# Router logits taken from rows that are not yet normalised, with gates, tables and tile addresses moved

## The chip, the core and the metric

The kernel runs on one core of one Trainium2 chip. The metric is device time in microseconds (us), the median over runs; lower is better. Five engines work in parallel from their own in-order queues: TensorE (PE in the profile, its weight loads PEld), VectorE (DVE), ScalarE (ACT), GpSimd (POOL) and SyncE (SP), which here issues the weight transfers.

## What is computed

256 tokens of width 1024 in float32 go through two blocks. Shortened from the reference:

```python
h = layer_norm(ALPHA * x + hybrid_mixer(x), ln1_g, ln1_b)        # first block
logits = h @ router_w + router_b                                 # 32 experts
top_vals, top_idx = lax.top_k(logits, 4); gates = softmax(top_vals)
# each expert: up (1024 -> 2048), gated activation, down (1024 -> 1024), for its tokens
h = layer_norm(ALPHA * h + moe(h), ln2_g, ln2_b)
u = rmsnorm(h)                                                   # second block
h = h + hybrid_mixer_2(u)   # projections, a scan over chunks of 128 with decays per head
h = h + conv_gated_mlp(rmsnorm(h)); return rmsnorm(h)
# the decays of the scan, for each of 32 heads:
decay_in = exp(where(causal, a_cum[l] - a_cum[s], -inf))
```

## The kernel before

**Projections.** Each float32 product is made of three matmuls (`mm3`, L163 to L165): activations and weights are split into a high and a low part, and high-high, high-low and low-high are added in PSUM. ACT rounds the high part of a weight chunk (tile wh, L61), DVE or POOL subtracts for the low one (wl, L158). In `units_t` a unit is 128 output columns: the weights are stationary and the 256 tokens stream past. In `units_n` it is the other way round. Activations lie in pairs of tiles: xth/xtl, soh/sol and hq/hk in the first mixer; uth/utl, xT, utx/yl0, ln/bc and yah/yal in the second block. `drive` runs the units in the order of a written list, and after every unit `tick` lets one side task (hgrn, attention, ssd, ...) take a step, up to its next `yield`.

By the built program, units_t issues 864 such matmuls with xth/xtl streaming, 192 with soh/sol and hq/hk, 1752 with uth/utl, 384 with xT, 384 with utx/yl0 and ln/bc, and 1056 with yah/yal; units_n issues 384 in the first mixer (w_out) and 192 in the second (w_o), and the last down projection 264 of 512 columns. The program also tells where each tile begins in a partition's memory. Modulo 512 bytes: the tiles wh and wl at 448 in the first mixer, at 64 in the second block; xth/xtl, soh/sol and hq/hk at 448; uth/utl, xT, utx and ln at 192; yl0, bc, yah and yal at 0. Of all the pairs that a matmul reads, only yah/yal with wh/wl have the activations at 0 and the weights at 64.

**Router.** The last units of the first mixer (w_out) end in `on_out` (L694, L696), which adds the residual to the rows xs block by block (256 columns) and takes statistics. `route` then normalises the rows (L789), transposes them on PE (L797), applies gain and bias (L800), multiplies by the router weights (L807), folds the four partial sums (L823) and picks the top four (L831 to L838). Three matmuls (L840 to L842) turn the choice into positions (L845), from which DVE builds a one-hot (L1059). The rows are split in hh and hl (ACT, and POOL at L816), and `gather` (L1021) multiplies them with the one-hot.

**Experts.** `some(0, 16)` and `some(16, 32)` go through the experts, 4 up chunks and 2 down chunks of 2 MB each, streamed by SP into eight slots: six of the rings and two of the tile lp, which also holds ln1's rows and the transposed rows while `route` runs, so that the second lp slot is handed over after it. After expert 0's up matmuls (L969) come `gates` (L858 to L877) and the slots of expert 0 (L987 to L992); `overflow_tables` (L889 to L936) follows as a side task from expert 1. `between(k)` runs after each of the eight k of an up projection; at k = 1 it issues the transposes of the expert before (`act_t`, L960), the sum into the result (`combine`, L1008) and the next slots.

**Decays.** In `ssd_near`, for each head, PE multiplies a one-hot column (selh, 64 partitions) with the running sums (ahl, 64 partitions: high and low part), 384 columns (L1437), and adds a mask (L1438) before ACT takes the exponent.

Of the kernel before, what the change touches and what calls it, by code (L numbers as in the profile page):

```python
# [28 lines left out]
P = 128  # L29
# [392 lines left out]
def mixer_1(g, xs, st, params, more, then):  # L422
# [3 lines left out]
    with ExitStack() as c:  # L426
# [6 lines left out]
        pa = c.enter_context(tc.tile_pool(name="m1pa", bufs=4, space=PSUM))  # L433
        lv = q.tile([P, 7, P], F32)
# [256 lines left out]

        def on_out(j, pt):
            s = slice(j, j + T)
# [4 lines left out]
        first = list(ut(2048, 512, on_hf))  # L698
        gates_u = [*ut(3584, 1024, copy_to(gs)), *ut(4608, 1024, copy_to(gh))]
        drive(g, [first[0], own, *first[1:], *ut(1536, 512, on_hq), *ut(3072, 512, on_hg),  # L700
                  lambda: g.tasks.append(hgrn()),
                  *un(1024, 512, copy_to(vs, False)), step, *un(2560, 512, copy_to(hv, False)), step,
                  *ut(512, 512, copy_to(sk)), step, *ut(0, 512, copy_to(sq, scale=0.125)), step,
                  *gates_u[:2], start_sb, *gates_u[2:],
# [3 lines left out]
                  *units_n(g, A["w_out"][0], 0, D, mg, sp, pj, on_out)], then)  # L708

# [6 lines left out]
def moe_params(g, p, land, pa):  # L716
# [24 lines left out]
    r.gb = turn_rows(g, rows, n, p, pa, "gb")  # L741
    r.b_up = p.tile([P, D], F32R, name="bup")
# [4 lines left out]
    r.fold = p.tile([P, NE], F32, name="fold")  # L747
    nc.vector.tensor_reduce(r.fold, g.ident.rearrange("p (r e) -> p e r", r=4), axis=mybir.AxisListType.X, op=OP.add)
# [4 lines left out]
    r.ones = p.tile([P, P], F32, name="ones")  # L753
    nc.vector.memset(r.ones, 1.0)
# [14 lines left out]
def route(g, h, st, lp, p, pu_, pd_, pc_):  # L769
# [4 lines left out]
    ln = lp[:, WIDE:WIDE + 2 * D].rearrange("p (a d) -> p a d", a=2)  # L774
    gam, bet = bcast_row(g, ln[:, 0], "ln1_g"), bcast_row(g, ln[:, 1], "ln1_b")
    hT = lp[:, WIDE + 2 * D:].rearrange("p (k t) -> p k t", k=8)
    add_ring(g, lp, 0, 1, WIDE)
    n = len(g.ahead)
    g.ahead += [fetch(g, *src) for src in (up_src(A, 0) + up_src(A, 1))[n:n + 1]]
    r.hh = p.tile([P, 2, D], F32R, name="hh")  # L780
    r.hl = p.tile([P, 2, D], F32R, name="hl")
    mv = p.tile([P, 2, 3], F32, name="mv")
    for tt in range(2):
        nc.vector.bn_aggr(mv[:, tt, :2], st[:, tt])
    rsqrt(g, mv[:, :, 2:3], mv[:, :, 1:2], 1e-5)
    for b in range(4):
        s = slice(b * T, b * T + T)
        for tt in range(2):
            nc.vector.tensor_scalar(h[:, tt, s], h[:, tt, s], mv[:, tt, 0:1], mv[:, tt, 2:3],  # L789
                                    op0=OP.subtract, op1=OP.mult)  # L790

    pl = pd_.tile([P, T], F32, name="pd")
    for b in range(4):
        pt = pu_.tile([P, 4, T], F32, name="pu")[:, :2] if b % 2 else pc_.tile([P, 2, T], F32, name="pc")
        for k in (2 * b, 2 * b + 1):
            for tt in range(2):
                nc.tensor.transpose(pt[:, k % 2, tt * P:tt * P + P], h[:, tt, k * P:k * P + P], g.ident)  # L797
        for k in (2 * b, 2 * b + 1):
            if k in (3, 5, 7):
                nc.vector.tensor_scalar(hT[:, k], pt[:, k % 2], r.gb[:, k:k + 1], r.gb[:, 8 + k:9 + k],  # L800
                                        op0=OP.mult, op1=OP.add)
            else:
                g.act(hT[:, k], pt[:, k % 2], AF.Identity, scale=r.gb[:, k:k + 1], bias=r.gb[:, 8 + k:9 + k])
        for k in (2 * b - 2, 2 * b - 1) if b < 3 else range(4, 8):
            if k >= 0:
                q = k % 4 * NE
                nc.tensor.matmul(pl[q:q + NE], r.rw[:, k], hT[:, k], start=k < 4, stop=k >= 4,  # L807
                                 skip_group_check=True, tile_position=(0, q))

    hv = h.rearrange("p t (q k) -> p t k q", k=8)  # L810
    hhv, hlv = (x.rearrange("p t (k q) -> p t k q", k=8) for x in (r.hh, r.hl))
    for b in range(2):
        s = slice(b * 4, b * 4 + 4)
        for tt in range(2):
            g.act(hhv[:, tt, s], hv[:, tt, s], AF.Copy)
            nc.gpsimd.tensor_sub(hlv[:, tt, s], hv[:, tt, s], hhv[:, tt, s])  # L816
    nc.gpsimd.tensor_mul(h[:, 0], h[:, 0], gam)
    nc.gpsimd.tensor_add(h[:, 0], h[:, 0], bet)
    lT = p.tile([P, 4 * P], F32, name="lT")[:, :T]
    nc.vector.tensor_copy(lT, pl)  # L820
    lg = pd_.tile([P, 2, NE], F32, name="pd")
    for tt in range(2):
        nc.tensor.matmul(lg[:, tt], lT[:, tt * P:tt * P + P], r.fold, start=True, stop=True)  # L823
    L = p.tile([P, 2, NE], F32, name="L")
    nc.vector.tensor_add(L, lg, r.rb[:, None, :].to_broadcast([P, 2, NE]))
# [1055 lines left out]
```

## Time and profile before

| | |
|---|---|
| median of 3 runs | 1806.98 us (1804.88 to 1809.86) |
| profiled execution | 1805.9 us, its span 1804.1 us |
| PE busy | 1680.7 us, 93% of the span |
| DVE, ACT, POOL busy | 42%, 31%, 9% |
| 244 to 266 us (router) | PE 12.60 of 22 us, granted clock 0.76 of full |
| 385 to 740 us (experts) | PE 329.49 of 355 us, transfers at 425 GB/s |
| 1225 to 1330 us (second block) | PE 101.35 of 105 us, DVE 72.86 |
| 1422 to 1638 us | PE 208.14 of 216 us, DVE 142.14 |
| 1638 to 1804 us | PE 158.58 of 166 us, DVE 98.55 |

The first mixer runs to 244 us, the router to 266, the experts to about 1208, the second block to the end. Busy is the time an engine spends in instructions; matmuls overlap, so that their rate is read from the distances between their starts.

### The profile page before, as it was taken

How to read it: one execution, taken by the hardware profiler on the slowest of the kernel's cores; microseconds unless marked ns; L12 is line 12 of the kernel's file. 1: busy time of each engine (PE TensorE's matmuls, PEld its weight loads, DVE VectorE, ACT ScalarE, POOL GpSimd, SP SyncE). 2: the span in 40 equal slices, each digit the busy share in tenths (PEclk: the TensorE clock that was granted, in tenths of full speed). 3: DMA queues.
4: the chain of work that ended last, by engine and by line, in shares of the span. 5: the costliest groups of instructions: out<-in, count | busy, mean ns of one | idle time of the engine just before them, and what ended most of it. 6: DMA issues, size and time to landing. Idle time of an engine off the chain costs nothing.

```text
span 1804.1 us, 23870 instructions
## 1 busy us (share of the span) xinstructions
PE 1680.7 (93%) x10102; PEld 1077.5 (60%) x10102; DVE 749.7 (42%) x1154; ACT 554.5 (31%) x858; POOL 158.2 (9%) x120
## 2 busy tenths in 40 slices
PE   6999979999999999899999999989999999999998
PEld 6998853333333333333333333348998899998997
DVE  4765462212211212122122121246766757566665
ACT  4547431010010100101001011016665456345454
POOL 4311230000000000000000000015201300021000
PEclk9999988999999999899999999999999999999999
DMA  9440858999999999899999999994543355545552
GB/s 304 132 149 16 309 210 328 424 418 428 428 427 427 428 428 427 375 428 427 427 428 429 425 428 428 427 334 131 185 141 117 118 187 187 168 165 170 193 183 92
DMA packets 149933, 535.60 MB, mean 297 GB/s; under 512 B 7123, under 2 KB 119139, under 8 KB 125504
## 3 DMA queue, kind: packets, MB, share of 16 engines
q1 hardware_dynamic: 147488, 529.68, 75.0%
q0 software_dynamic: 2048, 4.23, 0.7%
q8 instruction: 80, 1.31, 0.3%
q14 instruction: 29, 0.24, 0.0%
q10 hardware_dynamic: 288, 0.13, 0.0%
HBM read 532.97 MB, written 1.05 MB: 296 GB/s over the span
## 4 chain that ended last, share of the span: by engine, by line
PE 50%; DVE 4%; issue 2%; ACT 1%; POOL 1%; DMA 0%; DVEq 0%; ACTq 0%; POOLq 0%
PE pu L969 13%; PE pj L163 7%; PE pj L165 7%; PE pj L164 7%; PE pd L978 6%; PE pc L1008 2%; PE pa L164 1%; PE pa L165 1%; PE pa L163 1%; DVE xs L1010 1%; PE pc L1021 1%; POOL wl L158 1%; PE pa L1437 1%; PE px L960 1%; PE pu L1074 1%
## 5 line engine op out<-in xcount | busy, mean ns | idle before, releaser
L969 PE MATMUL pu<-ring,xt 128*64 128x512 f32 x1568 | 362.2, 613 | 1.3 <-ACT xt L61 1.3
L158 DVE TENSOR_TENSOR wl<-ring,wh 128x1024 fp32r<-128x1024 f32 (+1 forms) x224 | 269.8, 1228 | 51.5 <-ACT wh L61 51.2
L61 ACT ACTIVATE wh<-ring 128x1024 fp32r<-128x1024 f32 (+1 forms) x247 | 252.1, 1027 | 97.9 <-PE pj L164 41.7
L969 PEld LDWEIGHTS pu<-ring,xt 128*64 128x64 f32 x1568 | 110.3, 141 | 215.4 <-issue 208.9
L1010 DVE TENSOR_TENSOR xs<-xs,pc 128x512 f32<-128x512 f32 x124 | 79.7, 683 | 336.9 <-PE pc L1008 336.9
L947 DVE TENSOR_SCALAR xg<-pu 128x512 f32<-128x512 f32 x32 | 22.1, 691 | 360.1 <-PE pu L969 360.1
L163 PE MATMUL pj<-uth,wh 128*128 128x256 f32 x584 | 166.8, 286 | 0.0
L165 PE MATMUL pj<-uth,wl 128*128 128x256 f32 x584 | 164.8, 282 | 1.9 <-DVE wl L158 1.9
L164 PE MATMUL pj<-utl,wh 128*128 128x256 f32 x584 | 164.4, 281 | 0.0
L158 POOL TENSOR_TENSOR wl<-ring,wh 128x1024 fp32r<-128x1024 f32 x22 | 58.4, 2656 | 1105.2 <-ACT wh L61 1082.0
L978 PE MATMUL pd<-ring,act 128*64 128x512 f32 x704 | 154.8, 592 | 0.0
L61 ACT ACTIVATE sg<-xg 128x512 f32<-128x512 f32 x32 | 20.1, 630 | 350.8 <-DVE xg L947 350.8
L1008 PE MATMUL pc<-y,gpt 64*128 64x512 f32 x248 | 89.1, 645 | 24.9 <-DVE xs L1010 24.0
L165 PEld LDWEIGHTS pj<-uth,wl 128*128 128x128 f32 x584 | 110.0, 188 | 2.5 <-DVE wl L158 2.5
L163 PEld LDWEIGHTS pj<-uth,wh 128*128 128x128 f32 x584 | 110.0, 188 | 2.2 <-issue 2.1
L978 PEld LDWEIGHTS pd<-ring,act 128*64 128x64 f32 x704 | 50.4, 137 | 100.7 <-issue 100.7
L969 PE MATMUL pu<-lp,xt 128*64 128x512 f32 x480 | 110.4, 609 | 0.0
L164 PEld LDWEIGHTS pj<-utl,wh 128*128 128x128 f32 x584 | 110.0, 188 | 0.1
L163 PE MATMUL pj<-yah,wh 128*128 128x256 f32 x352 | 97.6, 277 | 0.0
L164 PE MATMUL pj<-yal,wh 128*128 128x256 f32 x352 | 97.4, 277 | 0.0
L165 PE MATMUL pj<-yah,wl 128*128 128x256 f32 x352 | 97.4, 277 | 0.0
L163 PE MATMUL pj<-xth,wh 128*128 128x256 f32 x288 | 84.3, 293 | 8.7 <-ACT wh L61 8.7
(440 smaller groups left out, 2853.4 us busy)
## 6 DMA issues: line engine op xcount, KB each, us to landing
ring<-in_expert_w_up_dram SPq DMA_DIRECT2D x98, 2048.0 KB, 19.9
ring<-in_expert_w_down_dram SPq DMA_DIRECT2D x44, 2048.0 KB, 18.4
ring<-in_w_in_dram SPq DMA_DIRECT2D x62, 1024.0 KB, 5.4
lp<-in_expert_w_up_dram SPq DMA_DIRECT2D x30, 2048.0 KB, 17.9
lp<-in_expert_w_down_dram SPq DMA_DIRECT2D x18, 2048.0 KB, 19.8
ring<-in_w_up_dram SPq DMA_DIRECT2D x22, 1024.0 KB, 5.2
ring<-in_w_down_dram SPq DMA_DIRECT2D x11, 1024.0 KB, 4.9
ring<-in_w_s_out_dram SPq DMA_DIRECT2D x8, 1024.0 KB, 5.0
```

What stands on the lines that cost most here:

```text
L61: self.nc.scalar.activation(out, x, func, **kw)
L158: return (hi_t, lo_t), lambda: (engine or g.nc.vector).tensor_sub(lo_t, src, hi_t)
L163: nc.tensor.matmul(out, a[0][asl], b[0][bsl], start=first, stop=False, skip_group_check=True)
L164: nc.tensor.matmul(out, a[0][asl], b[1][bsl], start=False, stop=False, skip_group_check=True)
L165: nc.tensor.matmul(out, a[1][asl], b[0][bsl], start=False, stop=last, skip_group_check=True)
L947: nc.vector.tensor_scalar(xg, pv[:, :, 0], 7.0, None, op0=OP.min)
L960: g.nc.tensor.transpose(pt[:, k], xv[:, k], g.ident)
L969: g.nc.tensor.matmul(pu[hf * 64:hf * 64 + 64, b], x, ch[:, hf * D + b * 512:hf * D + b * 512 + 512], start=first, stop=last, skip_group_ch ...
L978: g.nc.tensor.matmul(pd[n * 64:n * 64 + 64], act[:, k, hf], ch[:, s:s + 512], start=hf + k == 0, stop=hf * 4 + k == 7, skip_group_check=True)
L1008: nc.tensor.matmul(pc, gpt[s, tt], y[s], start=True, stop=True)
L1010: nc.vector.tensor_add(o, o, pc)
L1021: g.nc.tensor.matmul(pt[:, j], part[:, tt, (k + j) * P:(k + j + 1) * P], onehot(tt), start=tt + i == 0, stop=tt + i == 2)
```

## The change

Four things are edited. (1) The logits are formed from the rows as `on_out` leaves them: with the gain folded into the router weights, logits = rstd x (rows @ (gain x w)) - rstd x mean x (column sums of gain x w) + (bias @ w + b). `turn(b)` transposes a block of the rows and `dots(b)` multiplies it, between the w_out units; `logits` finishes after the last. The three constants are made in `moe_params` with 16 matmuls of 32 columns, in two further steps. `route` no longer transposes; the rows are normalised in four pieces by `first_rows`, and their split in hh and hl follows piece by piece, the low part on DVE. ln1's rows get a tile of their own, so both lp slots are handed over at once. (2) `gates` goes into expert 2's up projection piece by piece (`begin`), with the slots of experts 0 and 1 and the first `combine`; the overflow tables start after expert 4, in smaller steps. (3) selh and ahl get 128 partitions, the further 64 of them zero. (4) Pads of 72 and 16 floats in the first mixer, and dsk and dtn as the first tiles of the second block, move the tiles behind them: by the built program every activation pair of the projections then begins at 0 modulo 512 bytes, and wh and wl at 64, in both mixers.

```diff
@@ mixer_1
+        p.tile([P, 72], F32, name="pad")
+        sp.tile([P, 16], F32, name="pad", bufs=1)
...
+        def turn(b):
...
+            pt = pa.tile([P, 2, T], F32, name="pa")
+            for j in range(2):
+                for tt in range(2):
+                    nc.tensor.transpose(pt[:, j, tt * P:tt * P + P],
+                                        xs[:, tt, (2 * b + j) * P:(2 * b + j + 1) * P], g.ident)
+            g.act(rt["h"][:, 2 * b], pt[:, 0], AF.Copy)
+            nc.vector.tensor_copy(rt["h"][:, 2 * b + 1], pt[:, 1])
+
+        def dots(b):
+            for k in (2 * b, 2 * b + 1):
+                for tt in range(2):
+                    nc.tensor.matmul(rt["l"][:, tt], rt["h"][:, k, tt * P:tt * P + P], g.moe.rw[:, k],
+                                     start=k + tt == 0, stop=k == 7 and tt == 1, skip_group_check=True)
+
         def on_out(j, pt):
...
+            if b:
+                turn(b - 1)
             for tt in range(2):
-                nc.vector.bn_stats(st[:, tt, j // T], xs[:, tt, s])
+                nc.vector.bn_stats(st[:, tt, b], xs[:, tt, s])
+            if b > 1:
+                dots(b - 2)
+
+        def logits():
+            r = g.moe
+            turn(3)
+            dots(2)
+            mv = r.mv
+            for tt in range(2):
+                nc.vector.bn_aggr(mv[:, tt, :2], st[:, tt])
+            rsqrt(g, mv[:, :, 2:3], mv[:, :, 1:2], 1e-5)
+            dots(3)
+            first_rows(g, xs, mv)
...
@@ moe_params
+    for k in range(8):
+        nc.tensor.matmul(pt[:, 0, :NE], r.gb[:, 8 + k:9 + k].to_broadcast([P, P]), r.rw[:, k], start=k == 0,
+                         stop=k == 7)
...
+    for k in range(8):
+        nc.tensor.matmul(pt[:, 0, :NE], r.ones, r.rw[:, k], start=k == 0, stop=k == 7)
@@ route
+    add_ring(g, lp, 0, 2, WIDE)
...
+    high(0)
...
+    low(0)
+    first_rows(g, h, mv, 2)
+    high(2)
...
+    def more_rows():
+        low(2)
+        for k in (4, 6):
+            first_rows(g, h, mv, k)
+            high(k)
+        for k in (4, 6):
+            low(k)
+
     def rest():
-        nc.vector.tensor_mul(h[:, 1], h[:, 1], gam)
-        nc.vector.tensor_add(h[:, 1], h[:, 1], bet)
-    return rest
+        for tt in range(2):
+            nc.gpsimd.tensor_mul(h[:, tt], h[:, tt], gam)
+            nc.gpsimd.tensor_add(h[:, tt], h[:, tt], bet)
@@ experts
-                    if e == 0:
-                        gt = gates(g, acc, p, px, pc_)
-                        next(gt)
-                        at_slots(e)
-                        next(gt)
-                        g.tasks.append(overflow_tables(g, p, pc_))
...
+        begin = {0: lambda: next(gt), 2: lambda: next(gt), 3: lambda: next(gt),
+                 4: lambda: at_slots(0), 5: lambda: combine(g, acc, pc_, y.pop(0), gpt.pop(0)),
+                 6: lambda: at_slots(1)}
@@ second
+        dsk = p.tile([P, NH // 2], F32)
+        dtn = p.tile([P, 2, NH], F32)
...
-        selh = p.tile([64, NH], F32R)
+        selh = p.tile([P, NH], F32R)
...
-                sel = selh[:, hd:hd + 1].to_broadcast([64, P])
+                sel = selh[:, hd:hd + 1].to_broadcast([P, P])
```

How the order changes. On PE, from the end of the last w_out unit to the first gather matmul (ident is the identity of a transpose, gh the transposed rows, pd/pc/pu/pa/po are PSUM tiles). Before:

```order
L797 MATMUL pc<-ident,xs 128x128 x4
L797 MATMUL pu<-ident,xs 128x128 x4
L807 MATMUL pd<-lp,rw 32x256 x2
L797 MATMUL pc<-ident,xs 128x128 x4
L807 MATMUL pd<-lp,rw 32x256 x2
L797 MATMUL pu<-ident,xs 128x128 x4
L807 MATMUL pd<-lp,rw 32x256 x4
L823 MATMUL pd<-fold,lT 128x32 x2
L840 MATMUL pd<-mask,lt 128x32
```

Now, from the same place:

```order
L705 MATMUL pa<-ident,xs 128x128 x4
L713 MATMUL po<-rw,gh 128x32 x4
L705 MATMUL pa<-ident,xs 128x128 x4
L713 MATMUL po<-rw,gh 128x32 x8
L879 MATMUL pd<-mask,lt 128x32
```

Half of the transposes and a quarter of the products (not shown) now stand between the w_out units before this place, and the fold is gone.

On DVE, from the statistics to the one-hot of the first four experts. Before:

```order
L784 BN_AGGR mv<-st 128x2 x2
L789 TENSOR_SCALAR xs<-xs,mv 128x256 x8
L800 TENSOR_SCALAR lp<-pu,gbc 128x256
L800 TENSOR_SCALAR lp<-pc,gbc 128x256
L800 TENSOR_SCALAR lp<-pu,gbc 128x256
L820 COPY lT<-pd 128x256
L825 TENSOR_TENSOR L<-pd,rb 128x64
```

Now:

```order
L708 COPY gh<-pa 128x256
L732 BN_AGGR mv<-st 128x2 x2
L839 TENSOR_SCALAR xs<-xs,mv 128x2x128 x2
L736 SCALAR_TENSOR_TENSOR mv<-mv 128x2
L738 SCALAR_TENSOR_TENSOR L<-sums,mv,rb 128x32 x2
L740 SCALAR_TENSOR_TENSOR L<-po,mv,L 128x32 x2
```

Only a quarter of the rows is normalised ahead of the choice; the other six such operations, and the low parts hl, now stand behind the mask or behind the one-hot.

On PE, after the last up matmul of expert 0. Before:

```order
L990 MATMUL px<-ident,gp 128x128 x2
L870 MATMUL px<-ident,gate 32x128 x2
L875 MATMUL pc<-bd,lT 128x512 x4
L1074 MATMUL pu<-bup,pick 128x512 x2
L969 MATMUL pu<-ring_1959,xt 64x512 x8
L960 MATMUL px<-ident,xg 128x128 x4
L990 MATMUL px<-ident,gp 128x128 x2
L894 MATMUL pc<-mask,ones 128x32 x2
L913 MATMUL pc<-ident,ob 33x128
L969 MATMUL pu<-ring,xt 64x512 x8
```

Now:

```order
L1130 MATMUL pu<-bup,pick 128x512 x2
L1023 MATMUL pu<-ring_1983,xt 64x512 x8
L1014 MATMUL px<-ident,xg 128x128 x4
L1023 MATMUL pu<-ring,xt 64x512 x8
L1023 MATMUL pu<-lp,xt 64x512 x16
```

The gate matmuls now stand in expert 2, with up matmuls of one k between them, and the table matmuls in experts 5 to 10.

## Rows read from the trace of the kernel before

**Rows 1.** Busy time in three stretches; columns: stretch, length, each engine, granted clock, DMA share, GB/s.

```profile
70.00:110.00 40.00, 36.32 (x298) 35.16 (x299) 37.99 (x48) 16.68 (x20) 15.34 (x12) 1.00 0.33 107
110.00:210.00 100.00, 100.00 (x779) 94.54 (x778) 48.15 (x66) 60.91 (x101) 8.16 (x10) 1.00 0.41 137
1330.00:1422.00 92.00, 92.00 (x656) 75.68 (x656) 61.49 (x100) 52.68 (x127) 17.46 (x6) 1.00 0.40 122
```

**Rows 2.** Timeline of PE, first and last of four runs; columns: start, length, instruction.

```profile
160.85 0.28 PE L165 MATMUL pj<-xth,wl 128*128 128x256 f32 x1
...
163.36 0.28 PE L165 MATMUL pj<-xth,wl 128*128 128x256 f32 x1
...
1379.32 0.28 PE L164 MATMUL pj<-utl,wh 128*128 128x256 f32 x1
...
1381.93 0.28 PE L165 MATMUL pj<-uth,wl 128*128 128x256 f32 x1
...
1484.97 0.28 PE L165 MATMUL pj<-yah,wl 128*128 128x256 f32 x1
...
1491.77 0.28 PE L165 MATMUL pj<-yah,wl 128*128 128x256 f32 x1
...
1565.77 0.28 PE L163 MATMUL pj<-utx,wh 128*128 128x256 f32 x1
...
1570.13 0.28 PE L163 MATMUL pj<-utx,wh 128*128 128x256 f32 x1
```

**Rows 3.** Timeline of PE: decays of two heads, and attention's 384-column matmul on 128 partitions.

```profile
153.61 0.39 PE L582 MATMUL pa<-sbl,neg_tri 128*128 128x384 f32 x1
153.84 0.22 PE L583 MATMUL pa<-sbl,neg_one 128*128 128x128 f32 x1
...
1387.76 0.43 PE L1437 MATMUL pa<-ahl,selh 64*128 64x384 f32 x1
1388.12 0.39 PE L1438 MATMUL pa<-neg_big,identr 128*128 128x256 f32 x1
1388.44 0.44 PE L1437 MATMUL pa<-ahl,selh 64*128 64x384 f32 x1
1388.81 0.38 PE L1438 MATMUL pa<-neg_big,identr 128*128 128x256 f32 x1
1389.03 0.28 PE L163 MATMUL pj<-uth,wh 128*128 128x256 f32 x1
```

**Rows 4.** Timelines of ACT, DVE and PE from the end of w_out to the experts.

```profile
233.32 1.28 ACT L55 ACT_TABLE_LOAD   x1
...
253.07 4.17 ACT L61 ACTIVATE hh<-xs 128x512 fp32r<-128x512 f32 x4
...
243.76 0.69 DVE L694 SCALAR_TENSOR_TENSOR xs<-xs,pj 128x512 f32<-128x512 f32 x1 [1.40 <-PE pj L165]
...
246.34 2.67 DVE L789 TENSOR_SCALAR xs<-xs,mv 128x256 f32<-128x256 f32 x8 [0.69 <-ACT mv L61]
...
255.61 0.23 DVE L825 TENSOR_TENSOR L<-pd,rb 128x64 f32<-128x64 f32 x1 [0.72 <-PE pd L823]
...
256.44 2.48 DVE L836 TENSOR_TENSOR oh<-io,i 128x128 f32<-128x128 f32 x2
...
254.94 0.63 PE L823 MATMUL pd<-fold,lT 128*128 128x32 f32 x4 [0.52 <-DVE lT L820]
...
266.13 3.37 PE L969 MATMUL pu<-ring,xt 128*64 128x512 f32 x8 [0.66 <-ACT xt L61]
```

**Rows 5.** Timeline of PE after expert 0's up projection.

```profile
287.06 5.29 PE L875 MATMUL pc<-bd,lT 32*128 32x512 f32 x8 [0.45 <-ACT lT L871]
...
293.43 5.09 PE L969 MATMUL pu<-ring,xt 128*64 128x512 f32 x16
...
302.99 0.30 PE L913 MATMUL pc<-ident,ob 128*33 128x128 f32 x1 [2.30 <-DVE ob L911]
```

**Rows 6.** The tile lp: time from the issue of a weight transfer to its landing.

```profile
DMA to landing us min/median/max: 7.2/18.6/30.8
```

More of the change, by code (lines that the diff above doesn't have):

```diff
@@ L690, in on_hgb @@
             nc.gpsimd.tensor_sub(mg[1][:, s], gs[:, s], mg[0][:, s])
+        rt = {}
+        def turn(b):
+            if not rt:
+                rt["h"] = p.tile([P, 8, T], F32, name="gh")
+                rt["l"] = pa.tile([P, 2, NE], F32, name="po", bufs=1)
+            pt = pa.tile([P, 2, T], F32, name="pa")
[5 more added lines that the diff above has]
+            nc.vector.tensor_copy(rt["h"][:, 2 * b + 1], pt[:, 1])
@@ L695, in on_out @@
             for tt in range(2):
-                nc.vector.bn_stats(st[:, tt, j // T], xs[:, tt, s])
+                nc.vector.bn_stats(st[:, tt, b], xs[:, tt, s])
[11 more added lines that the diff above has]
+            first_rows(g, xs, mv)
+            nc.vector.scalar_tensor_tensor(mv[:, :, 3:4], mv[:, :, 0:1], -1.0, mv[:, :, 2:3], op0=OP.mult, op1=OP.mult)
+            for tt in range(2):
+                nc.vector.scalar_tensor_tensor(r.L[:, tt], r.sums, mv[:, tt, 3:4], r.rb, op0=OP.mult, op1=OP.add)
+            for tt in range(2):
+                nc.vector.scalar_tensor_tensor(r.L[:, tt], rt["l"][:, tt], mv[:, tt, 2:3], r.L[:, tt],
+                                               op0=OP.mult, op1=OP.add)
@@ L701, in mixer_1 @@
                   lambda: g.tasks.append(hgrn()),
[L702 removed]
+                  *un(1024, 512, copy_to(vs, False)), step, *hv_u[:2], step, *hv_u[2:], step,
                   *ut(512, 512, copy_to(sk)), step, *ut(0, 512, copy_to(sq, scale=0.125)), step,
[L704 removed]
+                  *gates_u[:2], step, start_sb, *gates_u[2:],
                   gates_done,
@@ L708, in mixer_1 @@
                   *units_n(g, A["w_out"][0], 0, D, mg, sp, pj, on_out)], then)
+        logits()
 NE = 32
@@ L766, in moe, with rows_of, first_rows, route @@
         drop_ring(g, lp)
-def route(g, h, st, lp, p, pu_, pd_, pc_):
+def rows_of(h, k):
+    return h.rearrange("p t (q k) -> p t k q", k=8)[:, :, k:k + 2]
+def first_rows(g, h, mv, k=0):
+    v = rows_of(h, k)
+    for tt in range(2):
+        g.nc.vector.tensor_scalar(v[:, tt], v[:, tt], mv[:, tt, 0:1], mv[:, tt, 2:3], op0=OP.subtract, op1=OP.mult)
+def route(g, h, st, lp, p, wp, pd_):
     nc, tc, A = g.nc, g.tc, g.A
     r = g.moe
-    ln = lp[:, WIDE:WIDE + 2 * D].rearrange("p (a d) -> p a d", a=2)
+    add_ring(g, lp, 0, 2, WIDE)
+    n = len(g.ahead)
+    g.ahead += [fetch(g, *src) for src in (up_src(A, 0) + up_src(A, 1))[n:n + 2]]
+    ln = p.tile([P, 2, D], F32, name="ln")
@@ L785, in route @@
[L785 to L808, printed above, removed]
@@ L820, in route, with high, low @@
[L820 to L825, printed above, removed]
+    hhv, hlv = (x.rearrange("p t (k q) -> p t k q", k=8) for x in (r.hh, r.hl))
+    def high(k):
+        g.act(hhv[:, :, k:k + 2], rows_of(h, k), AF.Copy)
+    def low(k):
+        nc.vector.tensor_sub(hlv[:, :, k:k + 2], rows_of(h, k), hhv[:, :, k:k + 2])
@@ L1055, in experts, with gather_group @@
         xt, act, gpt, y, pick = {}, {}, {}, {}, {}
-        def gather_group(e0):
+        def gather_group(e0, then=None):
             onehot = wp.tile([P, 2, GE, CAP], F32R, name="oneh", bufs=1)
@@ L1061, in gather_group @@
                                     op=OP.is_equal)
+            if then is not None:
+                then()
             for x in gather(g, r, lambda tt: onehot[:, tt].rearrange("p e s -> p (e s)"), GE * CAP, wp, pc_):
@@ L1069, in picks, with bias @@
             nc.vector.tensor_copy(pick[e], r.sel[:, e, :, None].to_broadcast([P, 2, CAP]))
-        def bias(e):
+        def bias(e, e0=None):
             pu = pu_.tile([P, 2, 512], F32, name="pu")
@@ L1076, in bias @@
                                  skip_group_check=True)
-            if e + 1 < NE:
+            if e + 1 < NE and e != e0:
                 picks(e + 1)
@@ L1125, in some @@
         def some(e0, e1):
-            first = gather_group(e0)
-            pu = bias(e0)
+            first = gather_group(e0, more_rows if e0 == 0 else None)
+            pu = bias(e0, e0)
             next(first)
@@ L1136, in between @@
                         next(first)
+                    if e == e0 and k == 5:
+                        picks(e + 1)
+                    if e == 2 and k in begin:
+                        begin[k]()
                     if k != 1:
```

67 lines of the change are left out of this document (36 added, 31 removed).

## The prediction

> **What bounds the kernel now.** I read the page first: PE is busy 1680.7 of 1804.1 us, 93%, and no other engine comes near half. So three things can shorten this kernel: PE's matmuls following each other faster, fewer stretches in which PE waits, and fewer at a reduced clock. I then went through the span by stages. Between 385 and 740 us PE is busy 329.49 of 355 us, and the transfers move 425 GB/s beside it; in the projections it is busy all the time, 100.00 of 100 us between 110 and 210, and 92.00 of 92 between 1330 and 1422 [rows 1]. The exceptions are 70 to 110 us, where DVE is busy 37.99 of 40 us and PE stands still for some of the time [rows 1], and the router, where PE is busy 12.60 of 22 us at a granted clock of 0.76.
>
> A PE that is always busy need not be at its best, since every matmul lasts 0.28 us in the timeline and overlaps its neighbours. I therefore measured from start to start, over runs without a gap [rows 2]: 21 distances with xth take 2.51 us, 0.1195 each; 22 with uth take 2.61 us, 0.1186; 36 with utx and yl0 take 4.36 us, 0.1211; and 60 with yah and yal take 6.80 us, 0.1133. All four stream 256 columns against 128x128 weights at full clock. What sets the fourth apart, as far as the program tells, is where its tiles begin in memory: activations at 0 and weights at 64 modulo 512 bytes.
>
> **Addresses.** All pairs now begin as the fourth does. If that is what makes it faster, the first mixer gains 0.1195 - 0.1133 = 0.0062 us on 864 + 192 matmuls of units_t, 6.5 us, and, if units_n gain like the others (I take 0.0055), 384 x 0.0055 = 2.1 us: 8.6 us. The 298 matmuls between 70 and 110 us lie under DVE [rows 1], so 298 x 0.0062 = 1.8 us of this turn into waiting; I take 6.5 us. The second block gains 1752 x 0.0053 = 9.3 us with uth, 384 x 0.0053 = 2.0 us with xT, 384 x 0.0078 = 3.0 us with utx and ln, and 192 x 0.005 = 1.0 us in units_n: 15.3 us. There DVE is busy 61.49 of 92 us beside the decays [rows 1], and less than 70% in the other stages of my table, so most of this should survive; I take 13. Together **-19.5 us**, with bounds of nothing and -24.
>
> The rows [rows 2] thus show a matmul whose pace differs by 4 to 7% with nothing different but tiles and place. The Trainium skill, page "TensorE: Matmul & The Clock Gate", section "Step-by-step: what each phase is for", says that the streamed operand and the weight load read through two independent ports, so that loading the next weights takes nothing from the running matmul. By that the address of one against the other would be indifferent, and this term 0 instead of -19.5. The trace shows at least that something separates the runs; that it is the address is inferred.
>
> **Constants of the router.** In moe_params 16 matmuls of 32 columns are added. The nearest row is the fold's four of 32 columns, 0.63 us [rows 4], so 16 take 2.5 us, or up to 3.5 if each waits for its weights; they fall into or near the stage where PE waits for DVE, so part is free: +1.5 us. Two `turn` (8 transposes) and one `dots` (4 products) move in front of the last w_out unit, where PE is the bound: 12 short instructions at about the 0.12 us of a 256-column one, with an entry from one form into another here and there, +1.7 us. Two further DVE copies where the second block's constants are made: +0.7 us. Together **+3.9 us**, bounds 2 and 6.
>
> **From the last w_out add to the first expert matmul.** That is 243.76 to 266.13 us, 22.4 us [rows 4]. The chain is DVE, PE and ACT in turns: 2.67 us for eight normalise operations ahead of the transposes, then transposes, gain and bias, products, fold (0.63 us), then the choice from 255.61, then the one-hot, two operations in 2.48 us, and the split, gather and its copy up to 266.13 [rows 4]. Now only two of the eight normalise operations stand ahead of the choice (saves 2.0 us), half of the transposes and their copies are done earlier, gain, bias and fold are gone. On the other side four things come in: the table load on ACT (1.28 us), before at 233.32 under w_out, stands behind the last transposed copy and is exposed; a turn of 4 transposes and 12 small products still follow; the logits need five small DVE operations at about 0.23 us each (L825, [rows 4]); and the rows' pieces for hh, four in 4.17 us on ACT [rows 4], are interleaved with the normalising, so the first xt copies stand behind some of them. The one-hot operations are long (1.24 us each) where POOL subtracts beside them; with this moved to DVE I take 0.6 for both. Bottom-up I come to 15 to 18 us for the new chain. Gain 4.3 to 7 us; I take **-5.5 us**. As lp no longer holds these rows, the transfer into its second slot starts earlier. It was not late: lp's transfers land 7.2 to 30.8 us after issue [rows 6], and PE waits for none in the experts.
>
> **Gates and tables.** After expert 0's up projection PE waits 0.45 us for the logits of the gates and takes 5.29 us for eight 512-column matmuls; sixteen such up matmuls then take 5.09 us, and PE stands 2.30 us for the tables' operand [rows 5]. At the pace of the fourth run [rows 2], twice 0.1133 us for 512 columns, eight take 1.8 and sixteen 3.6 us. So 3.5 us are lost in the first, 1.5 in the second, another 1.5 in a second stretch like it, and 2.75 in the two waits: 9.2 us. Spread between the eight k of expert 2, each step of `gates` has an up projection's k, 3.6 us, to cover its DVE and ACT work, so these waits go; what can go wrong is one new dip of the clock in expert 2, 1.5 us, or the gates' results being late for `combine`. The experts' end is set by PE, and a chunk is there 3 us or more before its use even at the largest lag in [rows 6], so an earlier start carries through. **-8.5 us**, bounds -5 and -10.5.
>
> **Decays.** For each head the 64-partition matmul starts 0.36 us before its mask, the mask 0.32 us before the next head's matmul; but where the mask is followed by a 128-partition projection matmul the distance is only 0.22 [rows 3]. So entering the 64-partition form costs 0.32 - 0.22 = 0.10 us. Attention's 384 columns on 128 partitions start 0.23 us before what follows [rows 3], against 0.36: 0.13 us. Together 0.23 us for each of 32 heads, 7.4 us; with 384 columns at the pace of 0.1133 for 256, 0.17 us, it is 0.29 and 9.3 us. The Trainium skill, page "TensorEngine Tiling (Array Packing)", section "Key Properties", says that changing the tiling mode drains the engine; the rows agree, by 0.10 us on the way in. DVE at 61.49 of 92 us and ACT at 52.68 leave room [rows 1]. **-8 us**, bounds -5 and -9.3.
>
> **Sum.** -19.5 + 3.9 - 5.5 - 8.5 - 8 = -37.6 us. The profiled execution took 1805.9 us, 1.8 around its span, 1.1 below the median of 1806.98 and inside the spread of the runs. 1805.9 - 37.6 = 1768.3; the other way, 1806.98 - 37.6 = 1769.4. I say 1769.
>
> **The rivals.** First: the addresses are indifferent. The pace of the yah runs would then come from something else, say less traffic of ACT and DVE beside them. For it: the runs lie in different stages, and no run of before has the same tiles at two addresses. Against it: the same instruction with utx and yl0, 75 us later in the same block, is the slowest of the four [rows 2]. Time: 1769 + 19.5 = 1788. By the skill's rule on the two ports it would be this one.
>
> Second: the moved work gains only part. If the tail, the gates and the decays give half of their 22 us (ACT's queue delaying the first xt copies, a clock dip in expert 2, DVE late with the decays), the time is 1769 + 11 = 1780.
>
> Third, the other side: a beginning at 0 is what costs, and yah is fast for another reason. In the utx run one of three matmuls streams yl0, which begins at 0, and the run is 0.0025 us a matmul slower than uth's [rows 2]; put down to that third alone, it is 0.0075 us. On the 864 + 192 + 384 + 1752 + 384 = 3576 matmuls of units_t whose activations move to 0, that is +27 us; with the other terms, 3.9 - 22 = -18, the time is about 1815. It decides from 18 / 3576 = 0.005 us a matmul on. Against it: yah and yal both begin at 0 and are the fastest.
>
> Fourth: little comes of anything, because 70 to 110 us, the end of the experts and the second block turn to waits for DVE; then 1800 to 1808.
>
> **How the numbers follow.** The forecast, all four terms about as summed, has 0.70; the indifferent addresses 0.16; half the moved work 0.06; the slower one 0.04; little change 0.04. A measurement of this kernel can tell about 0.3%, 5.4 us, from no change. The first three are all faster by more than that: 0.92; slower 0.04, same 0.04. The forecast's own range is 1757 (all terms at their far bounds: -24 + 2 - 7 - 10.5 - 9.3 = -49) to 1779. Up to 1779 alone some 3 in 10 would be left out, so the range goes on through the indifferent addresses: 1757 to 1789.
>
> **What would show it.** Right: starts 0.113 us apart with xth and uth; the first up matmul 15 to 18 us after the last w_out add; no wait or half-clock stretch after expert 0's up projection, and gate matmuls of 0.23 us in expert 2; the decay's first matmul 0.17 to 0.23 us before its mask, the mask 0.22 before the next. Wrong: xth and uth still at 0.119 (then the first rival, and the error is 19.5 us), or at 0.125 and more (the third); PE waiting for DVE between 1330 and 1422 us or for ACT in front of the first xt; a second half of the experts that starts no earlier than before because a transfer is late.

## The result

The changed kernel took 1776.86 us (median of 4 runs, 1774.01 to 1786.23) against 1806.65 of the kernel before: a ratio of 0.9842, interval 0.9803 to 0.9881. Run once more beside other kernels it took 1780.45 (ratio 0.9855, 0.9839 to 0.9870); the median of its eight runs is 1778.9. So 26 to 30 us were won where 38 were forecast. The sign and the range of 1757 to 1789 held; the forecast's own part of that range ended at 1779, so the result lies at its edge. Most of the difference lies in one term, the addresses.

The profile after, in the views of [rows 1]: busy time in three stretches of the changed kernel (stretch, length, PE, PEld, DVE, ACT, POOL, granted clock, DMA share, GB/s).

```profile
70.00:110.00 40.00, 37.26 (x320) 36.56 (x320) 35.83 (x44) 15.14 (x17) 14.89 (x12) 1.00 0.34 106
110.00:210.00 100.00, 99.36 (x787) 93.74 (x787) 50.95 (x72) 60.36 (x100) 9.73 (x11) 1.00 0.43 147
1316.00:1400.00 84.00, 82.38 (x692) 75.39 (x691) 65.83 (x99) 54.56 (x133) 23.04 (x8) 1.00 0.42 126
```

PE is still busy nearly all the time. Beside the decays DVE is now busy 65.83 of 84 us, and PE is no longer without a pause.

The pace of the projections, as in [rows 2], is the surprise. The timeline of PE of the changed kernel in the z units of the second block (start, length, instruction; L1567 is one matmul in plain float32, which the profile has as two instructions):

```profile
1425.44 0.28 PE L163 MATMUL pj<-uth,wh 128*128 128x256 f32 x1
...
1426.74 0.28 PE L165 MATMUL pj<-uth,wl 128*128 128x256 f32 x1
1426.86 0.60 PE L1567 MATMUL pa<-sq,mean 128*128 128x256 f32 x2
...
1428.23 0.28 PE L165 MATMUL pj<-uth,wl 128*128 128x256 f32 x1
...
1438.09 0.28 PE L165 MATMUL pj<-uth,wl 128*128 128x256 f32 x1
1438.20 0.59 PE L1567 MATMUL pa<-sq,mean 128*128 128x256 f32 x2
...
1438.75 0.28 PE L164 MATMUL pj<-utl,wh 128*128 128x256 f32 x1
...
1439.93 0.28 PE L165 MATMUL pj<-uth,wl 128*128 128x256 f32 x1
```

The same instructions on the same tiles start 0.118 us apart (11 distances in 1.30 us), then, behind one foreign matmul, 0.1133 apart (87 in 9.86), and behind the next one 0.118 again (10 in 1.18). There is nothing between: in every run of matmuls of this profile the median distance is either 0.113 to 0.114 or 0.118, some 2000 matmuls at the first and 3000 at the second. A run keeps its level to its end, however long it is (766 matmuls in one case). The mean is 0.1159 in the first mixer (0.1199 before) and 0.1162 in the second block (0.1176 before). The yah/yal pairs of the last MLP, which had 0.1133 before, have 0.1178 in this profile, with the same addresses as before.

The kernel before had both levels too. Right behind the yah run of [rows 2], and behind the same kind of foreign matmul (there L1500), its trace goes on:

```profile
1495.29 0.59 PE L1500 MATMUL pa<-sq,mean 128*128 128x256 f32 x2
...
1495.83 0.28 PE L164 MATMUL pj<-yal,wh 128*128 128x256 f32 x1
...
1506.90 0.28 PE L165 MATMUL pj<-yah,wl 128*128 128x256 f32 x1
```

These are 94 distances in 11.07 us, 0.1178 each: the same pairs at the same addresses, 4 us after the run that the forecast was read from.

The decays, to be held against [rows 3]:

```profile
1370.65 0.38 PE L1495 MATMUL pa<-ident,xT 128*128 128x128 f32 x2
1370.79 0.42 PE L1504 MATMUL pa<-ahl,selh 128*128 128x384 f32 x1
1371.04 0.28 PE L1505 MATMUL pa<-neg_big,identr 128*128 128x256 f32 x1
1371.16 0.33 PE L1504 MATMUL pa<-ahl,selh 128*128 128x384 f32 x1
1371.33 0.28 PE L1505 MATMUL pa<-neg_big,identr 128*128 128x256 f32 x1
```

From a mask to the next decay matmul are 0.12 us (0.32 before), from that to its mask 0.17 (0.37 before): 0.40 us for the second head of a pair, where 0.23 a head had been forecast from the 0.22 and 0.23 of the nearest rows. With the first head, its entry and the transposes a pair saves 0.7 us.

From the last w_out add to the experts, as in [rows 4], timelines of ACT, DVE and PE, and two more rows of ACT:

```profile
244.48 1.28 ACT L55 ACT_TABLE_LOAD   x1
...
242.35 0.69 DVE L718 SCALAR_TENSOR_TENSOR xs<-xs,pj 128x512 f32<-128x512 f32 x1 [2.12 <-PE pj L165]
...
246.34 0.93 DVE L839 TENSOR_SCALAR xs<-xs,mv 128x256 f32<-128x256 f32 x2 [1.14 <-ACT mv L61]
...
248.75 0.47 DVE L875 TENSOR_TENSOR oh<-io,i 128x128 f32<-128x128 f32 x2
...
250.00 0.60 PE L879 MATMUL pd<-mask,lt 128*128 128x32 f32 x2 [4.25 <-DVE mask L877]
...
257.57 3.58 PE L1023 MATMUL pu<-ring,xt 128*64 128x512 f32 x8 [2.82 <-ACT xt L61]
...
254.93 2.14 ACT L61 ACTIVATE hh<-xs 128x512 fp32r<-128x512 f32 x2 [2.04 <-DVE xs L839]
256.97 1.01 ACT L61 ACTIVATE xt<-pc,gbx 128x256 f32<-128x256 f32 x2
```

15.2 us instead of 22.4. The table load is exposed as forecast (DVE's normalising waits 1.14 us for ACT's result), the one-hot takes 0.47 us instead of 2.48, and the last wait is 2.82 us for ACT: its last two pieces of hh, for which it had itself waited 2.04 us for DVE's normalising, stand ahead of the first xt.

The gates, before [rows 5], now in expert 2:

```profile
308.21 3.95 PE L927 MATMUL pc<-bd,lT 32*128 32x512 f32 x8
312.09 3.62 PE L1023 MATMUL pu<-ring,xt 128*64 128x512 f32 x8
315.65 0.44 PE L1044 MATMUL px<-ident,gp 128*128 128x128 f32 x2
...
319.78 1.72 PE L1062 MATMUL pc<-y,gpt 64*128 64x512 f32 x4 [0.77 <-DVE xs L1064]
```

The waits of 0.45 and 2.30 us are gone, but the half clock is back here: the granted clock is 0.50 from 312.10 to 315.50 us, and eight up matmuls in 3.62 us are 0.45 us each. It is the dip that the prediction had named as the possible loss. The eight gate matmuls before it take 3.95 us (5.29 before). lp's transfers still land in time, 8.1 to 31.2 us after issue against [rows 6]; one weight load waits 0.3 us for one of them, the matmuls for none:

```profile
DMA to landing us min/median/max: 8.1/16.9/31.2
```

### The profile page after: what moved, and what is told of

It is laid out like the page before. It is cut to its first block, busy times and chain, and to the rows that moved or that the text cites. A ratio compares the mean times of both kernels' runs of the same rounds, so it can differ in the third digit from the quotient of the medians.

```text
span 1774.6 us, 23967 instructions
## 1 busy us (share of the span) xinstructions
PE 1651.6 (93%) x10146; PEld 1066.3 (60%) x10146; DVE 748.1 (42%) x1164; ACT 556.7 (31%) x859; POOL 157.0 (9%) x118
## 4 chain that ended last, share of the span: by engine, by line
PE 49%; DVE 4%; issue 3%; ACT 2%; POOL 1%; DMA 0%; DVEq 0%; ACTq 0%; POOLq 0%
PE pu L1023 13%; PE pj L163 7%; PE pj L165 7%; PE pj L164 7%; PE pd L1032 6%; PE pc L1062 2%; PE pa L164 1%; PE pa L163 1%; PE pa L165 1%; DVE xs L1064 1%; PE pc L1075 1%; POOL wl L158 1%; PE pu L1130 1%; PE px L1014 1%; PE po L1517 0%
```

## The experiments

**One part alone, or all but one.** Four kernels, compared in the same way with the kernel before.

The addresses alone, in the kernel before:

```diff
+        p.tile([P, 16], F32, name="pad")
+        sp.tile([P, 16], F32, name="pad", bufs=1)
...
+        dsk = p.tile([P, NH // 2], F32)
+        dtn = p.tile([P, 2, NH], F32)
...
-        dsk = p.tile([P, NH // 2], F32)
...
-        dtn = p.tile([P, 2, NH], F32)
```

> The kernel before with only the fourth edit: tiles padded so that every activation pair begins at 0 and wh/wl at 64 modulo 512 bytes. Theory of the prediction (the address alone sets the pace, 0.1133 us from start to start everywhere): -19.5 us, about 1787. Theory now, read from the trace of the changed kernel (with these addresses the pace has two levels, 0.1133 and 0.1178, and which one a run of matmuls has depends on what stood between it and the run before): about half of that, -11 us give or take 6, and both levels are seen here too. If addresses are indifferent: 1806 to 1807 and paces as before.

Measured: 1795.95 us (1794.37 to 1797.69), ratio 0.9938 (0.9925 to 0.9951), so -10.8 us. The two levels are there: some 2700 matmuls at 0.113, 2300 at 0.118. So addresses are not indifferent, and they bring 11 us, not 19.5. The profile shows where: up to the last w_out matmul 5.3 us are won (243.4 to 238.1 us), behind the experts' last up matmul 8.3 (618.0 to 609.6 us), and the experts between, whose code is the same, take 3.1 us more (923.1 instead of 920.0), with 54.1 us at half clock in place of 47.3.

The decays alone, in the kernel before:

```diff
-        selh = p.tile([64, NH], F32R)
+        selh = p.tile([P, NH], F32R)
...
-        ahl = p.tile([64, 3 * P], F32R)
+        ahl = p.tile([P, 3 * P], F32R)
...
+            nc.vector.tensor_copy(selh[64:], g.ident[64:, :NH])
+            nc.vector.tensor_copy(ahl[64:], g.ident[64:, None, :64].to_broadcast([64, 6, 64]))
```

> The kernel before with only the third edit: selh and ahl on 128 partitions, the further 64 of ahl zero. By the prediction: 0.23 us for each of 32 heads, -8 us, about 1799. By the trace of the changed kernel, where two heads with their transposes take about 0.9 us instead of 1.6: -11 us, about 1796. If DVE or ACT is late with the decays instead: within 2 us of before.

Measured: 1799.56 us (1797.52 to 1800.87), ratio 0.9955 (0.9942 to 0.9967), -7.2 us. The matmuls themselves save more: from the first transpose of two heads to the matmul behind them are 0.89 us instead of 1.63 on the mean, 11.7 us for the 16 such pairs. Part of it is given back in the last of them. The waits of PE for DVE there, before and with this edit (waiting instruction, what it waits for, us, times, longest):

```profile
PE po L1450 <- DVE xT L1455: 1.2, 1, 1.2
```

```profile
PE po L1452 <- DVE xT L1457: 3.0, 1, 3.0
```

In this profile the granted clock is at half for 6.8 us in the stage behind that wait, where the kernel before has none. Behind the experts' last up matmul 8.5 us are won all the same (609.4 instead of 618.0); the experts again take more, by 2.9 us, with 53.9 us at half clock.

All but the addresses:

```diff
-        p.tile([P, 72], F32, name="pad")
-        sp.tile([P, 16], F32, name="pad", bufs=1)
+        p.tile([P, 56], F32, name="pad")
...
-        dsk = p.tile([P, NH // 2], F32)
-        dtn = p.tile([P, 2, NH], F32)
```

(dsk and dtn stand where they stood before.)

> The changed kernel with the fourth edit undone: all pairs modulo 512 bytes where they were before. If the addresses were worth the predicted -19.5 us: about 1796. If they are worth about half, because half of the matmuls run at the slower of two levels: 1777 + 11, about 1788. If they are indifferent: 1777. The paces of before should be back: 0.120 in the first mixer, about 0.119 with uth.

Measured: 1789.08 us (1784.11 to 1794.22), ratio 0.9893 (0.9875 to 0.9911): 8.6 to 12.2 us above the changed kernel's two medians, 10 above that of its eight runs. The paces of before are back, 0.1198 in the first mixer and 0.119 to 0.120 with uth, except in the last MLP: its nine yah runs have 0.1178, where the kernel before had 0.1133 at the same addresses. This profile also gives the first part by itself, at unchanged paces: the last matmul of w_out starts at 246.5 us (243.4 before), 3.1 us later, for the constants and the turns, and the first expert matmul follows 15.6 us behind it (22.7 before), 7.1 us sooner.

All but the gates and tables:

```diff
-                    if e == 2 and k in begin:
-                        begin[k]()
...
+                    if e == 0:
+                        gt = gates(g, acc, p, px, pc_)
+                        next(gt)
+                        at_slots(e)
+                        next(gt)
+                        next(gt)
+                        g.tasks.append(overflow_tables(g, p, pc_))
```

> The changed kernel with the second edit undone: gates, the slots of expert 0 and their matmuls stand behind expert 0's up projection again, and the overflow tables run from expert 1. By the prediction's term: +8.5 us, 1785. By the trace of the changed kernel, in which 8.6 us were won ahead of the experts and 14.9 by their end: +6.3 us, 1783. If the gain of the two kernels' experts came from where the clock happened to fall: within 2 us of the changed kernel.

Measured: 1783.98 us (1782.47 to 1793.58), ratio 0.9886 (0.9864 to 0.9907): 3.5 to 7 us above the changed kernel, 5 by the median of its eight runs. That is between the prediction's term and nothing. Its interval overlaps with those of the changed kernel, whose runs spread by several us, so the size is no sharper than that.

**Which distance counts.** Four kernels, each with one pair of places in the first mixer and another in the second block. Only the pads differ: their sizes, and an additional one in front of wh and wl of the second block. The first of the four, in which the pad ahead of the first mixer's weights goes and one of 48 floats comes ahead of the second block's:

```diff
-        sp.tile([P, 16], F32, name="pad", bufs=1)
...
+        sp.tile([P, 48], F32, name="pad", bufs=1)
```

> The changed kernel with other pads: weights at 0 modulo 512 bytes in the first mixer, as the activations, and at 256 in the second block. If weights and activations must not begin at the same place: 0.120 in the first mixer, as in the kernel before, where both stood at 448 (+3 us there). For 256 nothing is known: if only a distance other than 0 is wanted, 0.1133 and 0.1178 as with 64, about 1780 in all; if a distance of 64 is special, 0.119, +5 us more, 1785.

> The changed kernel with other pads: weights at 256 modulo 512 bytes in the first mixer and at 128 in the second block, activations at 0. If only a distance other than 0 is wanted: two levels, 0.1133 and 0.1178, in both, 1777. If 64 is special: 0.119 and more, +3 us in the first mixer and +5 in the second block, 1785. If the beginning of the activations at 0 is what counts and the weights' is not: as the changed kernel, 1777, and the same with weights at 0.

> The changed kernel with other pads: weights at 32 modulo 512 bytes in the first mixer and at 448 in the second block, activations at 0. So far the second level's faster pace was seen at a distance of 64 alone; 0, 128 and 256 gave 0.119 to 0.120. If the distance has to be exactly 64: 0.119 to 0.120 in both, about 1793. If it has to be small but not 0: 0.1133 and 0.1178 in the first mixer with 32, and in the second block with 448 (64 the other way round), 1777; with only one of them, 1782 to 1788.

> The changed kernel with other pads: activations at 192 and weights at 256 in the first mixer (again a distance of 64, at another place), activations at 0 and weights at 96 in the second block. If the distance alone counts: 0.1133 and 0.1178 in the first mixer as in the changed kernel, and about 0.119 in the second block (+10 us there, 1787). If activations have to begin at 0: 0.120 in the first mixer too, 1792. If a small distance other than 0 is enough: two levels in both, 1777.

Measured: 1794.24, 1793.68, 1784.99 and 1786.33 us. The mean distance of starts in each part:

| weights minus activations, modulo 512 bytes | where | mean us | levels seen |
|---|---|---|---|
| 0 (both at 448, kernel before) | first mixer | 0.1199 | 0.120 |
| 0 (both at 0) | first mixer | 0.1198 | 0.120 |
| 32 | first mixer | 0.1179 | 0.116 to 0.118 |
| 64 (0 and 64) | first mixer | 0.1159 | 0.113 and 0.118 |
| 64 (192 and 256) | first mixer | 0.1155 | 0.113 and 0.118 |
| 96 | second block | 0.1180 | 0.117 to 0.120 |
| 128 | second block | 0.1190 | 0.119 to 0.120 |
| 256 | first mixer | 0.1198 | 0.120 |
| 256 | second block | 0.1199 | 0.120 |
| 448 | second block | 0.1172 | 0.113 (rare) and 0.118 |

The distance counts, not the place: 192 and 256 give what 0 and 64 give. Of those tried 64 is the best, 0 and 256 the worst. Distances 32, 96, 128 and 448 were each tried at one place, in one profile. That 512 is the period is not shown: 0 and 256 give the same, and 256 would fit every row as well. At the same place in the last MLP, the timeline of PE with a distance of 256 (15 distances in 1.80 us, 0.120):

```profile
1650.02 0.28 PE L163 MATMUL pj<-yah,wh 128*128 128x256 f32 x1
...
1651.82 0.28 PE L163 MATMUL pj<-yah,wh 128*128 128x256 f32 x1
```

**What sets the level.** One matmul more, read by nobody, ahead of the last MLP's first down projection; then two further ones, ahead of the sk units and of the z units.

```diff
+        def flip():
+            nc.tensor.matmul(pj.tile([P, 2, T], F32, name="pj")[:, 0], mean, keep, start=True, stop=True)
...
-                    yield lambda: drain(g)
+                    yield lambda: (drain(g), flip())
```

> The changed kernel with one matmul more, of mean and keep in plain float32 and read by nobody, ahead of the first down projection of the last MLP. In the changed kernel four such matmuls (L1567) each turned the pace from one level to the other. If the pace is a state that is kept until something else stands between: the yah/yal runs behind it go from 0.1178 to 0.1133, about 800 matmuls x 0.0045 = -3.5 us, 1773. If the pace is set by the traffic of ACT and DVE in that stage or by the addresses: 0.1178 stays, +0.3 us.

> The kernel with one matmul more in the last MLP, with two further ones: ahead of the sk units of the first mixer and of the z units of the second block. If each turns the pace of all that follows until the next thing that stands between: about 300 matmuls net in the first mixer at 0.1133 instead of 0.1178 (-1.4 us), about 790 net in the second block (-3.6 us), and the -3.5 us of the last MLP; with 0.3 us for each added matmul -7.5 us against the changed kernel, 1769. If a pace belongs to a stage: no run of matmuls changes its pace there, 1777.

Measured: 1776.88 us (1774.77 to 1780.06) with one, 1780.48 (1775.33 to 1784.37) with three; neither is shown to differ from the changed kernel. In the first the last MLP has the faster level, 35 distances in 3.97 us, 0.1134, with the changed kernel's addresses and the same work around:

```profile
1639.82 0.28 PE L163 MATMUL pj<-yah,wh 128*128 128x256 f32 x1
...
1643.79 0.28 PE L165 MATMUL pj<-yah,wl 128*128 128x256 f32 x1
```

That looked like the expected effect, but the control below, without the matmul, has 0.1136 in the same place. So the added matmul isn't shown to be the cause there; what is shown is that the stage, its traffic and its addresses don't fix the pace. In the second kernel the matmul for the z units does what was expected, within one profile: 46 distances at 0.1178, the added matmul (here L1742), 118 at 0.1135.

```profile
1419.52 0.28 PE L165 MATMUL pj<-uth,wl 128*128 128x256 f32 x1
1419.64 0.60 PE L1742 MATMUL pj<-keep,mean 128*128 128x256 f32 x2
...
1420.20 0.28 PE L164 MATMUL pj<-utl,wh 128*128 128x256 f32 x1
...
1433.59 0.28 PE L165 MATMUL pj<-uth,wl 128*128 128x256 f32 x1
```

From there on the four foreign matmuls of the sums (L1567 in the changed kernel) turn the pace as ever, but each the other way round than in the changed kernel's first profile: 0.1178, 0.1136, 0.1178, 0.1134. Behind the added matmul of the last MLP, with waits of PE around it, the pace is 0.1178, and behind the one in the first mixer 0.1178 too, so there no gain came.

**Rows beside the decays.** What DVE and POOL do at the end of the decays in the changed kernel (timeline), and PE's wait behind it:

```profile
1382.13 0.56 DVE L1510 TENSOR_TENSOR dec<-dec,cb 128x384 f32<-128x384 f32 x1 [0.22 <-ACT dec L61]
...
1388.71 4.01 DVE L1510 TENSOR_TENSOR dec<-dec,cb 128x384 f32<-128x384 f32 x2 [0.84 <-ACT dec L61]
...
1389.58 10.84 POOL L1396 TENSOR_TENSOR xs<-xs,ln 128x1024 f32<-128x1024 f32 x4
```

```profile
PE po L1517 <- DVE xT L1522: 3.4, 1, 3.4
```

A decay's product takes DVE 0.56 us. The four that begin while an operation of POOL runs take 1.32, 2.76, 2.41 and 2.71 us, and each ends 0.41 to 0.42 us after that operation. In narrower windows the second of them and the operation of POOL beside it stand by themselves, ending at 1392.71 and 1392.30 us:

```profile
1389.95 2.76 DVE L1510 TENSOR_TENSOR dec<-dec,cb 128x384 f32<-128x384 f32 x1
...
1389.58 2.72 POOL L1396 TENSOR_TENSOR xs<-xs,ln 128x1024 f32<-128x1024 f32 x1
```

The experiment moves POOL's four operations behind the first group's sums:

```diff
-            gains()
             drain(g)
...
             summed.append(gr)
+            if gr == 0:
+                nc.gpsimd.tensor_copy(keep[:, :1], rn[:, 0, :1])
+                gains()
```

> The changed kernel with the four row operations of POOL (L1396, 10.8 us) moved from beside the last decays to behind the first group's sums in the z units. Beside them DVE's product of a decay (L1510) takes 2.0 to 2.5 us instead of 0.55, and PE waits 3.4 us for DVE; before the change it waited 1.2 us there. If POOL is what makes DVE late: that wait falls below 1 us, with it the half-clock stretch that followed it in most runs, -2 to -5 us against the changed kernel, about 1773. If DVE is late for its own work: the wait stays near 3 us, 1777; if the z units need DVE as much: the wait comes back there, 1777 to 1779.

> The changed kernel as it is, beside the one above. 1776 to 1778. If the pace follows from the order of the instructions alone, the paces of its runs of matmuls are those of the first profile; where PE has waited for something in between they may differ.

Measured: 1776.32 us (1771.30 to 1784.58), ratio 0.9833 (0.9807 to 0.9859), and the unchanged one beside it 1780.45 (1774.22 to 1782.15), 0.9855 (0.9839 to 0.9870). The intervals overlap, so no version is shown to beat the changed kernel. The wait is gone from its place and stands again where POOL now works, as the last of the three cases had it; the waits of PE between 1300 and 1600 us:

```profile
PE pa L1567 <- DVE sq L1563: 3.3, 1, 3.3
PE pj L164 <- DVE xT L348: 2.7, 1, 2.7
PE pa L1504 <- ACT dec L61: 0.7, 1, 0.7
```

At the end of the decays the last three products take 0.55 to 0.56 us again, and beside POOL's rows the sum that PE then waits for (L1563) takes 2.46 us instead of 0.42. That POOL beside DVE is what delays PE is thereby shown; where to put its 10.8 us at no cost is not.

The control is the kernel of the first profile, and its levels are others. In the first mixer the run of 94 at 111 us has 0.1135 instead of 0.1178. In the second block the run behind the 3.4 us wait starts at 0.1134 instead of 0.1178, and from there up to 1556 us every run is the other way round: behind the four L1567 it is 0.1178, 0.1136, 0.1178, 0.1134. The share of fast matmuls in the second block is 0.80 instead of 0.36, the mean 0.1142 instead of 0.1162. At 1556 us the two profiles come with 0.1134 and 0.1178, and behind four transposes without a wait both have 0.1178. Behind the wait of 0.7 us at 1318 us the two differ as well, 0.1178 and 0.1136, at full clock in both; behind the 3.4 us wait the control alone had a half-clock stretch. So behind a wait the level differed between executions; L1567 turned whatever level it met, and some other instructions led to the same level from either.

## Why the prediction was right, and where it missed

**Addresses, predicted -19.5, measured -10.8 alone and 9 to 12 when undone.** The mechanism held: the distance between the tiles' beginnings sets the pace, and the first rival (indifferent) and the third (a beginning at 0 costs) are refuted by the table. The size failed, at the step that took the 0.1133 of the yah run [rows 2] for the pace of that configuration. It was the better of its two levels, and the trace of before had the other one, 0.1178, at 1495.83 us. With the means of the changed kernel's first profile, 0.1199 to 0.1159 on 1440 matmuls of the first mixer (-5.8 us) and 0.1176 to 0.1162 on 3768 of the second block (-5.3), the term is -11.1; with the control's 0.1157 and 0.1142 it is -18.9. With the means of the addresses alone, 0.1162 and 0.1153, it is -5.3 and -8.7, or -14.0, and the profile has -5.3 and -8.3 in these two parts. All at 0.1133 would have been -23.9 by the prediction's own sums, of which it took 19.5. So the levels cost some 5 to 13 us of that, differently in each execution. In the profile of the addresses alone 13.6 us in these parts became 10.6 in the whole span, because the experts took 3.1 us more; whether the addresses have anything to do with that is not shown.

The Trainium skill, page "TensorE: Matmul & The Clock Gate", section "Step-by-step: what each phase is for", says that the streamed operand and the weights are read through two independent ports. The prediction took from it that no address of one against the other would matter. The runs show that one does: 0.120 us at a distance of 0 or 256, 0.1155 to 0.1159 at 64. What in the engine or the memory makes the difference is not shown.

**Constants and turns, +3.9.** The first mixer ends 3.1 us later with the old addresses, where 3.2 were in the sum; the 0.7 us for copies in the second block isn't seen (63.3 us from the last up matmul to the first with uth in the kernel before, 63.2 with the decays edit alone, which brings these copies).

**Tail, -5.5.** Measured -7.1, at the far bound. The normalising, the one-hot and the table load came as worked out; ACT's pieces of hh cost 2.82 us at the end.

**Gates and tables, -8.5.** Measured -5 (3.5 to 7). By expert 4 the trace shows 9.5 us (from the first up matmul to expert 4's bias 109.0 instead of 118.5 us), at the last up matmul 6.3. The difference is the table matmuls in experts 5 to 10 and dips of the clock there and in expert 2: the prediction had bounded the dip with 1.5 us and had not counted the tables' matmuls where they went. Its 3.6 us of cover for each step was twice too much: one k of an up projection is eight matmuls, 1.94 us in expert 2. Only 0.77 us of waiting for DVE came of it there.

**Decays, -8.** Measured -7.2. Two errors cancel: 0.37 us a head in the matmuls instead of 0.23, and 1.8 us more of waiting for DVE at the end with a half-clock stretch behind it. The sentence that DVE at 61.49 of 92 us leaves room [rows 1] was wrong for the last heads: the share over the stage hides that a product of DVE that begins beside an operation of POOL on the rows ends only behind it. In the kernel before three products took 2.43 to 2.76 us there, and PE waited 1.2 us.

**Sum.** +3.1 - 7.1 - 5 - 7.2 - 11 = -27.2 us, against -27.8 by the changed kernel's eight runs. The terms are known to a few us each, so an agreement this close is luck. The second rival (half of the moved work) gave a time of 1780, nearly the measured one, but it is not what happened: those three terms gave 19.3 of 22 us.

**The spread.** The same kernel took 1774 to 1786 us. Two things vary between its executions. One is the level of the paces: 0.0020 us on 3768 matmuls are 7.5 us between the two profiles of it. The other is the clock: from the first up matmul to the last the two profiles take 913.7 and 914.0 us, and three kernels whose code is the same there 917.1, 916.2 and 921.4, with 37.5, 37.8, 44.4, 43.8 and 55.8 us at half clock. If half of that time is lost, that is 0.2, 3.5, 3.2 and 9.2 us more than in the first, the difference to within 1.5 us. The clock also accounts for 7.5 us of pace leaving only 2.2 in the span (1774.6 and 1772.4): the control is at half clock for 6.8 us from 1400.7 and for 3.4 us from 1574.8, where the first profile is not, and half of these 10.2 us leaves 2.4. Why the clock falls more often in one execution stays open.

## What to carry to other kernels

Measure the pace of back-to-back matmuls from start to start, in several runs of them and in more than one execution: a pace seen in one stage may be the better of two levels, and of 23.9 us counted with it on all matmuls the paces of three executions gave 11 to 19 here. Where weights and activations begin in memory relative to each other is worth a few pads when PE is the bound: 256-column matmuls took 0.120 us with a distance of 0 or 256 bytes modulo 512 and 0.114 to 0.116 with 64. A busy share of two thirds does not mean that an engine can't be late: look for what runs on the other engines beside the instruction that the bound engine waits for.

## What the runs showed of the hardware that was not expected

A run of 256-column matmuls of `mm3` at full clock has one of two paces, 0.1133 or 0.1178 us, when its tiles begin 64 bytes apart modulo 512, and keeps it for up to 766 matmuls. L1567 (with other line numbers in other kernels), one float32 matmul between two runs, turned it in each of the four places, in both profiles of the changed kernel and in the five of other kernels with distance 64 in the second block, 28 of 28. The transposes between the w_o units turned it in some places and not in others. At a distance of 0 or 256 there was one pace, 0.120. What in the engine holds the level is open.

An element-wise operation of DVE with two inputs in SBUF that begins while one of POOL with two such inputs runs seems to stand until that one is over. In the changed kernel's first profile six products of 384 columns began so and ended 0.41 to 0.42 us behind POOL's operation (0.96 to 2.76 us in all, 0.54 to 0.56 alone). Eleven subtractions of 1024 columns ended 1.08 us behind it (1.45 to 3.36 us, 1.16 to 1.23 alone). The sixteen with one input in PSUM that began so were not held up: 0.68 to 0.69 us for 512 columns.
